# Batch norm, inference form: phases of three tiles instead of two, parameters loaded as rows, and stores held back in four phases

## The chip, the cores and the metric

The kernel runs on one core of a Trainium2 chip. The metric is device time in microseconds (us) of one execution; a median of several is quoted. Every execution below ran at a granted clock of 1.0, all the timed ones were in the fast state, and the single run of `before_again` has the state "unknown", as single runs have. Spreads are quoted.

## The reference

```
x: [32, 256, 128, 128] float32;  gamma, beta, running_mean, running_var: [256] float32
return gamma * (x - running_mean) / sqrt(running_var + 1e-5) + beta      # per channel
```

The input has 537 MB, and so has the output. With scale = gamma / sqrt(var + eps) and shift = beta - mean * scale, each element needs one multiply and one add.

## The kernel before

A tile is 128 channels of one image: 128 partitions x 16384 floats, 8.39 MB, 64 KiB for each partition. There are 64 tiles and three buffers in SBUF. All loads and stores are issued from the sync queue (SP); VectorE works in place. After three first loads the program goes in phases of two: two stores, two loads.

```python
    for i in range(NBUF):                      # NBUF = 3
        issue_load(i)

    def load_param(ap_1d):                     # 256 values, scattered in pieces of 4 bytes
        t = params.tile([P, NCB], mybir.dt.float32, tag=ap_1d.tensor.name)
        nc.gpsimd.dma_start(out=t, in_=ap_1d.rearrange("(j p) -> p j", p=P))
        return t
    # ... four such loads; sqrt on ScalarE, then scale and shift on VectorE [cut]

    K = NBUF - 1
    for b in range((NT + K - 1) // K):
        idxs = [i for i in range(K * b, K * b + K) if i < NT]
        for i in idxs:
            compute(i)                         # one tensor_scalar, in place
        for i in idxs:
            store(i)
        for i in idxs:
            issue_load(i + NBUF)               # waits until the buffer's store is done
```

Of the kernel before, what the change touches and what calls it, by code (L numbers as in the profile page):

```python
# [1 line left out]

# [4 lines left out]


SINGLE_QUEUE = True  # L10
NBUF = 3


@with_exitstack
def kernel(
    ctx: ExitStack,
    tc: tile.TileContext,
    x: bass.AP,
    gamma: bass.AP,
    beta: bass.AP,  # L20
    running_mean: bass.AP,
    running_var: bass.AP,
    out: bass.AP,
):
    nc = tc.nc
    eps = 1e-5

    N, C, H, W = x.shape
    P = nc.NUM_PARTITIONS
    assert C % P == 0  # L30
    NCB = C // P
    HW = H * W
    NT = N * NCB

    params = ctx.enter_context(tc.tile_pool(name="params", bufs=1))
    data = ctx.enter_context(tc.tile_pool(name="data", bufs=NBUF))

    xr = x.rearrange("n (cb p) h w -> (n cb) p (h w)", p=P)
    outr = out.rearrange("n (cb p) h w -> (n cb) p (h w)", p=P)

    tiles = {}
    loads = {}

    def issue_load(i):
        if i >= NT:
            return
        t = data.tile([P, HW], mybir.dt.float32, tag="t")
        loads[i] = nc.sync.dma_start(out=t[:], in_=xr[i])  # L48
        tiles[i] = t

    for i in range(NBUF):
        issue_load(i)

    def load_param(ap_1d):
        t = params.tile([P, NCB], mybir.dt.float32, tag=ap_1d.tensor.name)
        nc.gpsimd.dma_start(out=t, in_=ap_1d.rearrange("(j p) -> p j", p=P))  # L56
        return t

    var_t = load_param(running_var)
    gamma_t = load_param(gamma)  # L60
    beta_t = load_param(beta)
    mean_t = load_param(running_mean)

    eps_t = params.tile([P, 1], mybir.dt.float32, tag="eps")
    nc.vector.memset(eps_t, eps)  # L65

    scale_t = params.tile([P, NCB], mybir.dt.float32, tag="scale")
    shift_t = params.tile([P, NCB], mybir.dt.float32, tag="shift")
    tmp_t = params.tile([P, NCB], mybir.dt.float32, tag="tmp")

    nc.scalar.activation(  # L71
        out=tmp_t[:],
        in_=var_t[:],
        func=mybir.ActivationFunctionType.Sqrt,
        bias=eps_t[:],
        scale=1.0,
    )
    nc.vector.reciprocal(out=tmp_t[:], in_=tmp_t[:])  # L78
    nc.vector.tensor_mul(out=scale_t[:], in0=gamma_t[:], in1=tmp_t[:])  # L79
    nc.vector.tensor_mul(out=tmp_t[:], in0=mean_t[:], in1=scale_t[:])  # L80
    nc.vector.tensor_sub(out=shift_t[:], in0=beta_t[:], in1=tmp_t[:])  # L81

    def compute(i):
        t = tiles[i]
        cb = i % NCB
        nc.vector.tensor_scalar(  # L86
            out=t[:],
            in0=t[:],
            scalar1=scale_t[:, cb : cb + 1],
            scalar2=shift_t[:, cb : cb + 1],  # L90
            op0=mybir.AluOpType.mult,
            op1=mybir.AluOpType.add,
        )

    def store(i):
        t = tiles.pop(i)
        (nc.sync if SINGLE_QUEUE else nc.scalar).dma_start(out=outr[i], in_=t[:])  # L97

    K = NBUF - 1
    for b in range((NT + K - 1) // K):  # L100
        idxs = [i for i in range(K * b, K * b + K) if i < NT]
        for i in idxs:
            compute(i)
        for i in idxs:
            store(i)
        for i in idxs:
            issue_load(i + NBUF)


# [1 line left out]
_INS = ['x', 'gamma', 'beta', 'running_mean', 'running_var']  # L111
_OUTS = [((32, 256, 128, 128), 'float32')]


# [23 lines left out]
```

## Time and profile before

| | before |
|---|---|
| median of the first 3 runs | 2491.8 us (2489.71 to 2493.32) |
| span of the profiled run | 2488.1 us |
| moved | 1073.75 MB, mean 432 GB/s |
| VectorE busy | 23% |

From the page of the kernel before: the span, busy time, the DMA row and its rate in 40 slices of about 62 us, the main DMA queue (packets, MB, share of 16 engines' time), and the one costly group of instructions.

```profile
span 2488.1 us, 378 instructions
DVE 564.7 (23%) x69; ACT 1.6 (0%) x2; POOL 3.2 (0%) x8
...
DMA  9999999999999999999999999999999999999998
GB/s 414 429 438 433 433 429 437 436 430 431 435 436 433 428 437 436 434 428 436 433 437 428 435 435 435 426 437 436 435 427 435 436 438 426 434 437 436 432 431 378
...
q1 hardware_dynamic: 18432, 1073.75, 99.8%
...
L86 DVE TENSOR_SCALAR t<-t,scale_t,shift_t 128x16384 f32<-128x16384 f32 x64 | 564.0, 8812 | 1868.0 <-DMA t<-in_x_dram 1867.9
```

The DMA engines are busy throughout. VectorE needs 8.8 us for a tile and the DMA engines 19.3 us for each of its two transfers, so the idle 1868 us of VectorE cost nothing. The Trainium skill, page "DMA: Bandwidth & Descriptors", section "Where 436 GB/s comes from", gives 435.2 GB/s as the ceiling of the 16 ports into SBUF; the mean of 432 and the best slices of 438 (a slice holds a few packets too many or too few) agree with it.

The timeline of the first two phases (start us, duration us, engine or queue, line):

```profile
0.74 1.33 SPq L48 DMA_DIRECT2D t<-in_x_dram  x3
...
25.56 8.81 DVE L86 TENSOR_SCALAR t<-t,scale_t,shift_t 128x16384 f32<-128x16384 f32 x1
34.40 19.06 SPq L97 DMA_DIRECT2D out_dram<-t  x2
...
82.93 19.66 SPq L48 DMA_DIRECT2D t<-in_x_dram  x2
102.63 28.19 SPq L97 DMA_DIRECT2D out_dram<-t  x2
```

The first two stores are issued at 34 and 53 us, while the loads before them run until about 62 us. Work is always queued well ahead of the engines. Parameters that are ready only at 25.5 us delay nothing.

### How the small losses are read

The page cannot resolve 0.1%. The trace also holds a record of each packet (start, duration, bytes). A packet here is 64 KiB, the share of one partition. The records do not name the DMA engine, so packets were chained: each is put after the packet that ended as it started, which gives 16 chains, one for each engine. (Where two packets end in the same few ns, two chains may be swapped; sums over all chains are not touched by that, but a figure of the worst chain can be off by half a microsecond.) The median packet takes 2.418 us, 2.414 from start to start, so a chain of 1024 packets needs 2472 us. What a chain takes beyond 2.414 us per 64 KiB is called its loss. "Turn" is the point where a chain goes from loads to stores or back.

### The profile page before, as it was taken

To read this page: it belongs to the slowest core of one execution; us is meant where nothing else is said; L and a number is where in the kernel's file an instruction comes from. 1 tells how busy PE (TensorE), PEld (TensorE's weight loads), DVE (VectorE), ACT (ScalarE), POOL (GpSimd) and SP (SyncE) were. 2 spreads that over 40 slices of the span, in tenths; PEclk is the share of its full clock that TensorE was granted. 3 is DMA by queue.
4 is the path that set the end of the run, shared out by engine and by line. 5 is a ranking of instruction groups with operands and counts; after the bars stand their busy time and mean duration, and the time that the engine had idled before them with its cause. 6 is when DMAs were issued, how large, how long until landed. Compare 5 with 4: busy or idle time off the path is not lost.

```text
span 2488.1 us, 378 instructions
## 1 busy us (share of the span) xinstructions
DVE 564.7 (23%) x69; ACT 1.6 (0%) x2; POOL 3.2 (0%) x8
## 2 busy tenths in 40 slices
DVE  2122211222112221122212222121221212212121
ACT  0000000000000000000000000000000000000000
POOL 0000000000000000000000000000000000000000
DMA  9999999999999999999999999999999999999998
GB/s 414 429 438 433 433 429 437 436 430 431 435 436 433 428 437 436 434 428 436 433 437 428 435 435 435 426 437 436 435 427 435 436 438 426 434 437 436 432 431 378
DMA packets 18562, 1073.77 MB, mean 432 GB/s; under 512 B 2176, under 2 KB 2176, under 8 KB 2176
## 3 DMA queue, kind: packets, MB, share of 16 engines
q1 hardware_dynamic: 18432, 1073.75, 99.8%
q0 software_dynamic: 128, 0.00, 0.0%
q14 instruction: 2, 0.02, 0.0%
HBM read 536.88 MB, written 536.87 MB: 432 GB/s over the span
## 4 chain that ended last, share of the span: by engine, by line
DMA 51%; another core or an unknown queue 36%; DVE 11%; SPq 0%; issue 0%; POOL 0%; DVEq 0%; POOLq 0%; PEldq 0%
DMA t<-in_x_dram 48%; DVE t L86 11%; DMA out_dram<-t 2%; DMA t<-in_running_mean_dram 1%; SPq L97 0%; POOL t L56 0%; DVEq L86 0%; POOLq L133 0%; SPq L48 0%; DVE shift_t L81 0%; DVE tmp_t L80 0%; DVEq L80 0%; PEldq L133 0%
## 5 line engine op out<-in xcount | busy, mean ns | idle before, releaser
L86 DVE TENSOR_SCALAR t<-t,scale_t,shift_t 128x16384 f32<-128x16384 f32 x64 | 564.0, 8812 | 1868.0 <-DMA t<-in_x_dram 1867.9
L78 DVE RECIPROCAL tmp_t<-tmp_t 128x2 f32<-128x2 f32 x1 | 0.2, 166 | 13.2 <-ACT tmp_t L71 13.2
L80 DVE TENSOR_TENSOR tmp_t<-t,scale_t 128x2 f32<-128x2 f32 x1 | 0.2, 160 | 7.6 <-DMA t<-in_running_mean_dram 7.6
L71 ACT ACT_TABLE_LOAD x1 | 1.3, 1283 | 12.4 <-DMA t<-in_running_var_dram 12.4
L79 DVE TENSOR_TENSOR scale_t<-t,tmp_t 128x2 f32<-128x2 f32 x1 | 0.2, 160 | 3.2 <-DMA t<-in_gamma_dram 3.2
L56 POOL DMA_DIRECT2D t<-in_running_var_dram x1 | 0.8, 839 | 0.8 <-PEq L133 0.8
L56 POOL DMA_DIRECT2D t<-in_gamma_dram x1 | 0.7, 722 | 0.0
L56 POOL DMA_DIRECT2D t<-in_beta_dram x1 | 0.7, 722 | 0.0
L56 POOL DMA_DIRECT2D t<-in_running_mean_dram x1 | 0.7, 722 | 0.0
L71 ACT ACTIVATE tmp_t<-t,eps_t 128x2 f32<-128x2 f32 x1 | 0.3, 295 | 0.0
L65 DVE MEMSET eps_t<- 128x1 f32 x1 | 0.1, 59 | 0.8 <-PEq L122 0.8
L81 DVE TENSOR_TENSOR shift_t<-t,tmp_t 128x2 f32<-128x2 f32 x1 | 0.2, 160 | 0.0
L122 POOL MEMSET const-bfloat16-1.0<- 128x1 bf16 x1 | 0.1, 96 | 0.0
L122 POOL MEMSET const-uint8-127<- 128x1 uint8 x1 | 0.1, 94 | 0.0
L122 POOL MEMSET const-float32-0.0<- 128x1 f32 x1 | 0.1, 93 | 0.2 <-issue 0.2
L122 POOL MEMSET const-float32-1.0<- 128x1 f32 x1 | 0.1, 93 | 0.0
## 6 DMA issues: line engine op xcount, KB each, us to landing
t<-in_x_dram SPq DMA_DIRECT2D x64, 38.6
out_dram<-t SPq DMA_DIRECT2D x64, 49.9
t<-in_running_var_dram POOLq DMA_DIRECT2D x1, 1.0 KB, 11.1
t<-in_gamma_dram POOLq DMA_DIRECT2D x1, 1.0 KB, 15.2
t<-in_beta_dram POOLq DMA_DIRECT2D x1, 1.0 KB, 19.5
t<-in_running_mean_dram POOLq DMA_DIRECT2D x1, 1.0 KB, 21.6
```

The lines of the kernel that those rows point to most:

```text
L56: nc.gpsimd.dma_start(out=t, in_=ap_1d.rearrange("(j p) -> p j", p=P))
L65: nc.vector.memset(eps_t, eps)
L71: nc.scalar.activation(out=tmp_t[:], in_=var_t[:], func=mybir.ActivationFunctionType.Sqrt, bias=eps_t[:], scale=1.0,)
L78: nc.vector.reciprocal(out=tmp_t[:], in_=tmp_t[:])
L79: nc.vector.tensor_mul(out=scale_t[:], in0=gamma_t[:], in1=tmp_t[:])
L80: nc.vector.tensor_mul(out=tmp_t[:], in0=mean_t[:], in1=scale_t[:])
L81: nc.vector.tensor_sub(out=shift_t[:], in0=beta_t[:], in1=tmp_t[:])
L86: nc.vector.tensor_scalar(out=t[:], in0=t[:], scalar1=scale_t[:, cb : cb + 1], scalar2=shift_t[:, cb : cb + 1], op0=mybir.AluOpType.mult, ...
L122: nc = _bacc.Bacc("TRN2", target_bir_lowering=False, num_devices=1)
```

## The change

Its intent is to turn less often between reading and writing HBM (phases of three tiles use all three buffers), to load the parameters as four rows and transpose them on VectorE, and, in four of 22 phases, to keep the first store back until the DMA engine that lags has nearly finished the phase's loads.

```diff
+GROUPS = [3] * 20 + [2, 2]
+LAST = 3072
+HELD = (5, 10, 15, 20)
...
+    def load_group(g, first):
+        last = first + GROUPS[g] - 1
+        for i in range(first, last):
+            load(i, [HW])
+        if g not in HELD:
+            load(last, [HW])
+            return None
+        return load(last, [HW - LAST, HW])[0]      # 13312 columns, then 3072
...
-        nc.gpsimd.dma_start(out=t, in_=ap_1d.rearrange("(j p) -> p j", p=P))
+    rows = params.tile([B, C], f32, tag="rows")
+    nc.vector.memset(rows, 0.0)
+    for r, ap in enumerate((running_var, gamma, beta, running_mean)):
+        nc.scalar.dma_start(out=rows[r : r + 1, :], in_=ap.rearrange("(o c) -> o c", o=1))
+    # ... nc.vector.transpose and four small copies [cut]
...
+    for g, size in enumerate(GROUPS):
+        idxs = range(first, first + size)
+        for i in idxs:
+            compute(i)
+        for i in idxs:
+            s = store(i)
+            if i == first and gate is not None:
+                tc.add_manual_dep(s.ins, gate.ins.name, after, reason="stores after loads")
+        first += size
+        if g + 1 < len(GROUPS):
+            gate = load_group(g + 1, first)
```

More of the change, by code (lines that the diff above doesn't have):

```diff
@@ L7 @@
 from concourse._compat import with_exitstack
-SINGLE_QUEUE = True
 NBUF = 3
+GROUPS = [3] * 20 + [2, 2]
+LAST = 3072
+HELD = (5, 10, 15, 20)
 @with_exitstack
@@ L26 @@
     eps = 1e-5
+    f32 = mybir.dt.float32
     N, C, H, W = x.shape
@@ L33 @@
     NT = N * NCB
+    B = 32
+    NQ = P // B
+    assert sum(GROUPS) == NT and max(GROUPS) <= NBUF
     params = ctx.enter_context(tc.tile_pool(name="params", bufs=1))
@@ L39 @@
     outr = out.rearrange("n (cb p) h w -> (n cb) p (h w)", p=P)
+    ctx.enter_context(tc.manual_schedule())
     tiles = {}
-    loads = {}
-    def issue_load(i):
-        if i >= NT:
-            return
-        t = data.tile([P, HW], mybir.dt.float32, tag="t")
-        loads[i] = nc.sync.dma_start(out=t[:], in_=xr[i])
-        tiles[i] = t
-    for i in range(NBUF):
-        issue_load(i)
-    def load_param(ap_1d):
-        t = params.tile([P, NCB], mybir.dt.float32, tag=ap_1d.tensor.name)
-        nc.gpsimd.dma_start(out=t, in_=ap_1d.rearrange("(j p) -> p j", p=P))
-        return t
@@ L59, with load @@
-    var_t = load_param(running_var)
-    gamma_t = load_param(gamma)
-    beta_t = load_param(beta)
-    mean_t = load_param(running_mean)
-    eps_t = params.tile([P, 1], mybir.dt.float32, tag="eps")
-    nc.vector.memset(eps_t, eps)
-    scale_t = params.tile([P, NCB], mybir.dt.float32, tag="scale")
-    shift_t = params.tile([P, NCB], mybir.dt.float32, tag="shift")
-    tmp_t = params.tile([P, NCB], mybir.dt.float32, tag="tmp")
+    def load(i, cuts):
+        t = data.tile([P, HW], f32, tag="t")
+        tiles[i] = t, cuts
+        return [
+            nc.sync.dma_start(out=t[:, a:b], in_=xr[i][:, a:b])
+            for a, b in zip([0, *cuts], cuts)
+        ]
@@ new lines @@
+    gate = load_group(0, 0)
+    eps_t = params.tile([P, 1], f32, tag="eps")
+    nc.vector.memset(eps_t, eps)
+    turned = params.tile([B, C], f32, tag="turned")
+    nc.vector.transpose(out=turned[:], in_=rows[:])
+    par = params.tile([P, NCB, 4], f32, tag="par")
+    blocks = turned.rearrange("p (cb q r) -> p cb q r", cb=NCB, q=NQ)
+    for q in range(NQ):
+        nc.vector.tensor_copy(out=par[q * B : (q + 1) * B], in_=blocks[:, :, q, 0:4])
+    var_t, gamma_t, beta_t, mean_t = (par[:, :, r] for r in range(4))
@@ L71 @@
+    scale_t = params.tile([P, NCB], f32, tag="scale")
+    shift_t = params.tile([P, NCB], f32, tag="shift")
+    tmp_t = params.tile([P, NCB], f32, tag="tmp")
     nc.scalar.activation(
         out=tmp_t[:],
-        in_=var_t[:],
+        in_=var_t,
         func=mybir.ActivationFunctionType.Sqrt,
@@ L78 @@
     nc.vector.reciprocal(out=tmp_t[:], in_=tmp_t[:])
-    nc.vector.tensor_mul(out=scale_t[:], in0=gamma_t[:], in1=tmp_t[:])
-    nc.vector.tensor_mul(out=tmp_t[:], in0=mean_t[:], in1=scale_t[:])
-    nc.vector.tensor_sub(out=shift_t[:], in0=beta_t[:], in1=tmp_t[:])
+    nc.vector.tensor_mul(out=scale_t[:], in0=gamma_t, in1=tmp_t[:])
+    nc.vector.tensor_mul(out=tmp_t[:], in0=mean_t, in1=scale_t[:])
+    nc.vector.tensor_sub(out=shift_t[:], in0=beta_t, in1=tmp_t[:])
     def compute(i):
-        t = tiles[i]
+        t, cuts = tiles[i]
         cb = i % NCB
-        nc.vector.tensor_scalar(
-            out=t[:],
-            in0=t[:],
-            scalar1=scale_t[:, cb : cb + 1],
-            scalar2=shift_t[:, cb : cb + 1],
-            op0=mybir.AluOpType.mult,
-            op1=mybir.AluOpType.add,
-        )
-    def store(i):
-        t = tiles.pop(i)
-        (nc.sync if SINGLE_QUEUE else nc.scalar).dma_start(out=outr[i], in_=t[:])
-    K = NBUF - 1
-    for b in range((NT + K - 1) // K):
-        idxs = [i for i in range(K * b, K * b + K) if i < NT]
+        for a, b in zip([0, *cuts], cuts):
+            nc.vector.tensor_scalar(
+                out=t[:, a:b],
+                in0=t[:, a:b],
+                scalar1=scale_t[:, cb : cb + 1],
+                scalar2=shift_t[:, cb : cb + 1],
+                op0=mybir.AluOpType.mult,
+                op1=mybir.AluOpType.add,
+            )
+    def store(i):
+        t, _ = tiles.pop(i)
+        return nc.sync.dma_start(out=outr[i], in_=t[:])
+    after = mybir.DependencyInfo(mybir.DependencyClass.Sync, mybir.DependencyReason.DATA)
+    first = 0
+    for g, size in enumerate(GROUPS):
+        idxs = range(first, first + size)
         for i in idxs:
@@ L104 @@
         for i in idxs:
-            store(i)
-        for i in idxs:
-            issue_load(i + NBUF)
+            s = store(i)
[4 more added lines that the diff above has]
+            gate = load_group(g + 1, first)
 _INS = ['x', 'gamma', 'beta', 'running_mean', 'running_var']
```

## The prediction

> **What bounds the kernel now.** DMA, end to end. The page shows VectorE busy 23% and the DMA row at 9 tenths in all but the last slice; q1 takes 99.8% of 16 engines' time, 1073.75 MB at a mean of 432 GB/s over 2488.1 us. The Trainium skill, "DMA: Bandwidth & Descriptors", section "Where 436 GB/s comes from", puts the ceiling at 435.2 GB/s; this trace agrees (432 mean, best slices 438). Only the distance to that ceiling can be won.
>
> I read it from the packet records. Chaining each 64 KiB packet to the one that ended as it started gives 16 chains of about 1024 packets. The median packet takes 2.418 us (2.414 from start to start), so 1024 need 2472 us. The first starts at 1.8 us, the last ends at 2486.9: the worst chain loses about 13 us (0.5%), in two places:
> - 1.5 to 3.2 us in the first tile, whose packets take up to 4.7 us while the queue starts and the parameter packets pass (7 to 24 us);
> - about 10 us at turns from loads to stores: the last read packet before a turn takes up to 3.15 us, in some chains. One of the 32 turns costs the worst chain about 0.33 us on average. Turns from stores to loads cost almost nothing. Chains drift apart to 9.8 us.
>
> **What the change does.**
> - Three-tile phases: 22 such turns instead of 32. Estimate: 10 x 0.33 = 3.3 us less. The queue stays filled: a 19.3 us transfer covers the 8.8 us tensor_scalar (timeline).
> - Parameters as rows over the scalar queue, turned on VectorE: ready before the present 25.4 us (timeline, shift_t). Worth nothing in itself, as stores queue behind the three first loads (about 60 us); other small packets beside the first tile may save about 1 us.
> - Four held phases: the first store waits for the first 13312 columns of the last tile. The last engine still has 8 packets of 12 KiB then, about 3.6 us (3072/16384 of 19.3), against about 0.5 us from landing to a waiter's start plus 1 to 1.5 us from issue to first packet (0.74 to 1.76 us at the start). So the last engine should not idle; the leaders do, by up to their lead. That realigns the engines but gives the last one nothing back. As another engine may be last afterwards, the sum of the worst of each block (10.9 us in this trace cut into blocks at the holds) replaces the worst sum (9.9 us): about +1 us, less if aligned turns are cheaper.
> - Extra tensor_scalar pieces, SP waits, smaller packets: off the critical path.
>
> **Prediction.** -3.3 - 1 + 1 = -3.3 us on 2491.8: 2488.5 us, ratio 0.9987; range 2480 to 2495. Faster by over 2%: 0.01, within 2%: 0.98, slower by over 2%: 0.01. Over 2% would need more than the packets' own time allows.
>
> **What would show it.** Right: median packet still 2.418 us; DMA row at 9 throughout; late packets at 22 turns only, worst chain losing about 7 us there; shift_t ready before 20 us; the spread between chains dropping at the four holds, with idle time on leaders only. Wrong in size: rarer turns cost more each, or aligned turns nothing (nearer 2480).
>
> **What would make it wrong.** A hold that reaches the last engine too (a gap of 1 to 3 us, four times), a three-tile phase that empties the queue while SP waits for a buffer (a repeated dip of the DMA row), or packet times that change with the length of a run of reads or writes.

## The result, and the profile after

| | before | after |
|---|---|---|
| median, same rounds (and the 3 runs of before) | 2490.76 us (2485.85 to 2493.40, 6 runs) | 2492.29 us (2491.14 to 2493.93, 6 runs) |
| ratio after / before | | 1.0012, 95% interval 1.0001 to 1.0023 |
| span of the profiled run | 2488.1 us | 2489.8 us |

A ratio is the mean time of one kernel's runs over that of the other's in the same rounds, so it is not quite the ratio of the medians. By a difference whose interval only just leaves 1 out, the change did not gain the 3.3 us predicted: it lost about 1.5.

From the page after, the lines that answer to those above, and the new queue of the parameter rows:

```profile
span 2489.8 us, 388 instructions
DVE 566.7 (23%) x79; ACT 1.6 (0%) x2; POOL 0.2 (0%) x4
...
GB/s 421 432 427 438 438 433 426 438 436 434 428 437 432 427 436 434 437 426 437 436 426 425 433 437 437 430 431 438 422 438 421 437 432 430 437 437 434 426 431 397
...
q1 hardware_dynamic: 19008, 1073.75, 99.9%
...
q10 hardware_dynamic: 8, 0.00, 0.0%
```

The page says "full" as before: a late packet counts as busy. The few slices of 421 to 426 in the second half are a hint, no more.

The timeline after, at the start:

```profile
0.73 1.33 SPq L56 DMA_DIRECT2D t<-in_x_dram  x3
...
1.14 0.50 ACTq L74 DMA_DIRECT2D rows<-in_running_var_dram  x1
...
22.38 0.43 DVE L81 STREAM_TRANSPOSE turned<-rows 32x256 f32<-32x256 f32 x1 [21.25 <-DMA rows<-in_running_mean_dram]
```

The four rows of 1 KB land only at about 22 us, although they were issued by 2.5 us. Their eight packets (four of 1024 bytes, four of 4 bytes for the semaphore) start at 4.8, 7.3, 9.7, 12.1, 14.6, 17.0, 19.4 and 21.9 us: one for each 64 KiB packet of the tile loads. The Trainium skill, page "DMA: Bandwidth & Descriptors", section "Queues, rings and completion order", says that an engine goes round its queues packet by packet; the trace agrees, at 2.4 us a round.

The waits of the sync queue after (who waited for what: us in total, times, longest):

```profile
SPq L120 <- DVE t L109: 1228.6, 57, 47.1
SPq L56 <- DMA out_dram<-t: 962.8, 60, 19.1
SPq L120 <- DMA t<-in_x_dram: 214.0, 4, 53.7
```

The third line is the four holds. Now the first tensor_scalar of each phase, in the timeline of VectorE after. Its start is the moment when the phase's first load has landed on all engines, so the distance of two such lines is the length of a phase of three loads and three stores. The phase that begins at 1769.35 is held.

```profile
1653.25 8.81 DVE L109 TENSOR_SCALAR t<-t,scale_t,shift_t 128x16384 f32<-128x16384 f32 x1 [68.48 <-DMA t<-in_x_dram]
...
1769.35 8.81 DVE L109 TENSOR_SCALAR t<-t,scale_t,shift_t 128x16384 f32<-128x16384 f32 x1 [68.53 <-DMA t<-in_x_dram]
...
1885.84 8.81 DVE L109 TENSOR_SCALAR t<-t,scale_t,shift_t 128x16384 f32<-128x16384 f32 x1 [72.40 <-DMA t<-in_x_dram]
...
2003.58 8.81 DVE L109 TENSOR_SCALAR t<-t,scale_t,shift_t 128x16384 f32<-128x16384 f32 x1 [68.56 <-DMA t<-in_x_dram]
...
2119.75 8.81 DVE L109 TENSOR_SCALAR t<-t,scale_t,shift_t 128x16384 f32<-128x16384 f32 x1 [68.46 <-DMA t<-in_x_dram]
```

The phases take 116.10, 116.49 (held), 117.74 and 116.17 us. The held phase is nearly as short as the others; the one **after** it is 1.6 us longer. The same stands at the two holds before: 116.43 then 117.22, and 116.41 then 117.80.

The packet chains show the same in more detail. Loss of the mean chain, in us, at each hold of the changed kernel, and the time from the issue of the first held store to its first packet on the first and on the last chain:

```
hold   issue to first packet     at the held   next turn,      next turn,
       first chain  last chain   turn          stores->loads   loads->stores
1         1.6         3.2          0.07          0.25            0.82
2         0.9         3.2          0.36          0.57            1.13
3         0.8         3.2          0.68          0.68            1.28
4         0.8         3.2          0.42          0.68            1.23
```

Other turns from stores to loads lose 0.01 us, other turns from loads to stores about 0.1 us, but the very first one 1.03 us. The twelve entries add up to 8.2 of the 12.9 us that the mean chain loses.

Read chain by chain, the third hold shows more. The three chains that came last still had 2.2 to 3.2 us of loads before them when the stores were issued, and lost less than 0.1 us at the held turn: they did not run dry. At the next turn to loads they lost 0.01 us, but at the next turn to stores 1.7 to 1.9 us, more than any other chain. On every chain these two turns together cost 1.7 to 2.3 us. At the first hold no chain ran dry at all (all had 1.6 to 3.2 us left), and the two turns still cost the mean chain 1.1 us. So the later loss is not paid only by engines that stood idle.

### The profile page after: what moved, and what is told of

It is laid out like the page before. It is cut to its first block, busy times and chain, and to the rows that moved or that the text cites. A ratio compares the mean times of both kernels' runs of the same rounds, so it can differ in the third digit from the quotient of the medians.

```text
span 2489.8 us, 388 instructions
## 1 busy us (share of the span) xinstructions
DVE 566.7 (23%) x79; ACT 1.6 (0%) x2; POOL 0.2 (0%) x4
## 4 chain that ended last, share of the span: by engine, by line
another core or an unknown queue 72%; DVE 22%; issue 2%; DMA 2%; DVEq 0%; SPq 0%
DVE t L109 22%; DMA t<-in_x_dram 2%; DVEq L109 0%; SPq L56 0%
## 5 line engine op out<-in xcount | busy, mean ns | idle before, releaser
L109 DVE TENSOR_SCALAR t<-t,scale_t,shift_t 128x16384 f32<-128x16384 f32 (+2 forms) x68 | 564.7, 8310 | 1869.8 <-DMA t<-in_x_dram 1817.1
```

Source lines behind the costliest of these rows:

```text
L109: nc.vector.tensor_scalar(out=t[:, a:b], in0=t[:, a:b], scalar1=scale_t[:, cb : cb + 1], scalar2=shift_t[:, cb : cb + 1], op0=mybir.AluOpT ...
```

## The experiments

**Theory.** The hold costs, through lateness: the held stores reach engines that have no queued work left, or nearly none, and after so late a start about 1 us is lost at the next turn from loads to stores, as at the first turn of the changed kernel. **Rivals:** the cut load and its short packets cost; the gate costs whatever its lead; the loss belongs to three-tile phases; and, for the gain that was predicted, turns do cost in proportion to their number (the prediction) or do not. A further rival was not put to a run: engines that a hold has drawn together turn all at once and hinder one another. The trace of the changed kernel speaks against it: at its second turn to stores the chains are 0.8 us apart, closer than after any hold (1.6 us or more), and the mean chain loses 0.04 us.

Four kernels in each of three calls ran on the same chip (chips 1, 7 and 2 in turn) beside the same runs of the kernel before. A difference between calls therefore holds the chip as well. The table gathers all: medians of time, and from one trace of each the loss in us of the mean chain (in the first three tiles, later, and in all), of the worst chain, and how far apart the chains end.

```
kernel           time (lowest-highest)        ratio     first 3  later  mean   worst  ends apart
before           (33 runs, see below)                   2.3      5.1    7.4    13.1   9.2
after            2492.29 (2491.14-2493.93)    1.0012    1.7     11.2   12.9    14.7   2.4
call 1, before 2489.98 (2485.23-2492.58)
no_holds         2487.03 (2486.00-2488.17)    0.9992    1.7      3.7    5.4     8.5   4.8
split_only       2486.31 (2485.08-2486.55)    0.9988    2.0      3.6    5.6     9.0   5.6
all_held         2496.11 (2494.34-2496.74)    1.0027    1.4     15.6   17.0    18.6   3.0
rows_only        2486.45 (2486.02-2486.76)    0.9989    2.0      3.8    5.8     9.5   5.5
call 2, before 2487.24 (2486.41-2492.20)
gate_early       2486.36 (2486.08-2487.16)    0.9998    1.9      5.0    6.9     9.0   3.9
gate_late        2497.26 (2495.99-2498.95)    1.0041    1.7     16.8   18.6    19.1   0.8
hold_loads       2496.05 (2494.77-2496.89)    1.0036    1.9     14.7   16.5    19.0   2.8
one_tile         2487.24 (2485.88-2488.30)    0.9998    1.8      3.8    5.7    11.1   7.5
call 3, before 2487.55 (2486.77-2492.27)
before_again     2491.10 (one run)                      2.3      5.6    7.9    14.0   9.1
scatter_scalar   2500.09 (2499.34-2501.77)    1.0050   12.8      7.5   20.3    24.1   5.8
rows_gpsimd      2486.66 (2485.99-2487.25)    0.9994    1.8      3.8    5.6     9.0   5.5
late_params      2487.16 (2486.97-2492.24)    1.0000    2.3      3.8    6.1    10.1   6.2
```

### no_holds

```diff
-HELD = (5, 10, 15, 20)
+HELD = ()
```

> The changed kernel without any held phase (three-tile phases and row parameters stay). Turn theory of the prediction: about 3 to 4 us under the kernel before, ratio about 0.9985, about 1 us under the changed kernel. Hold-cost theory, from the changed kernel's trace (the held turn plus the two turns after it lose about 1.1, 2.1, 2.6 and 2.3 us on the mean chain, some 8 us in all, where unheld turns lose 0.1): about 2484 us, 7 to 8 us under the changed kernel, and no turn after the first with a mean loss over 0.4 us.

2487.03 us, 5.3 us under the changed kernel's median (other rounds; against the kernel before, 0.9992 instead of 1.0012). The timeline of VectorE in the same five phases as above:

```profile
1651.25 8.81 DVE L109 TENSOR_SCALAR t<-t,scale_t,shift_t 128x16384 f32<-128x16384 f32 x1 [68.43 <-DMA t<-in_x_dram]
...
1767.34 8.81 DVE L109 TENSOR_SCALAR t<-t,scale_t,shift_t 128x16384 f32<-128x16384 f32 x1 [68.56 <-DMA t<-in_x_dram]
...
1883.29 8.81 DVE L109 TENSOR_SCALAR t<-t,scale_t,shift_t 128x16384 f32<-128x16384 f32 x1 [68.47 <-DMA t<-in_x_dram]
...
1999.64 8.81 DVE L109 TENSOR_SCALAR t<-t,scale_t,shift_t 128x16384 f32<-128x16384 f32 x1 [68.47 <-DMA t<-in_x_dram]
...
2115.60 8.81 DVE L109 TENSOR_SCALAR t<-t,scale_t,shift_t 128x16384 f32<-128x16384 f32 x1 [68.39 <-DMA t<-in_x_dram]
```

The phases take 116.09, 115.95, 116.35 and 115.96 us: no long phase. At the same twelve turns the mean chain loses 0.9 us in all, against 8.2 with the holds. That difference of 7.3 is nearly the whole difference of the mean chains (12.9 - 5.4 = 7.5). The time differs by less, because the holds bring the chains together: they end 2.4 us apart instead of 4.8.

### split_only

```diff
-        return load(last, [HW - LAST, HW])[0]
+        load(last, [HW - LAST, HW])
+        return None
```

> The last load of the same four phases cut into 13312 and 3072 columns, but the stores not held. If the hold (the late stores) is what costs: as the kernel without holds, within 1.5 us, and the turns after the cut loads lose about 0.1 us. If the short 12 KiB packets or the extra transfer cost: as the changed kernel, with the losses of 0.3 to 1.3 us in the two turns after each cut.

2486.31 us, like the kernel without holds. The turns at the cut loads and the next ones to stores lost 0.03 to 0.26 us on the mean chain. The cut and the short packets cost nothing that shows here; the wait does.

### all_held

```diff
-HELD = (5, 10, 15, 20)
+HELD = tuple(range(22))
```

> All 22 phases held. Hold-cost theory with a cost of about 2 us per hold: 18 more holds, some 30 to 40 us over the changed kernel, ratio about 1.013 to 1.017. If the cost is one of drifting back into step after a hold and does not add up when every turn is held: under 12 us more. If holds cost only what the prediction said (the worst of the block): within 4 us of the changed kernel.

2496.11 us: 9 us over the kernel without holds, in the same rounds, and only 4 us over the changed kernel. So holds cost, but not by a fixed sum each: 22 of them cost 9 us, four cost 5. In this trace the turns from stores to loads lose 7.4 us in all (no_holds: 0.1) and those from loads to stores about 3 us, so the turns of about 1 us are gone where the next turn is itself held. The estimate of 30 to 40 us was wrong. By its figure alone the run fits the second and just the third of the outcomes written down; the third, that holds cost no more than the prediction said, is excluded by the 9 us over the kernel without holds. In this trace an expensive turn to stores follows a hold only where it is not held itself.

### rows_only

```diff
 # the kernel before, with
-    var_t = load_param(running_var)    # and gamma, beta, mean, through gpsimd
+    for r, ap in enumerate((running_var, gamma, beta, running_mean)):
+        nc.scalar.dma_start(out=rows[r : r + 1, :], in_=ap.rearrange("(o c) -> o c", o=1))
+    # ... transposed as in the change
```

> The kernel before with the parameters as rows and nothing else changed. Prediction: about 1 us faster than before, the first tile losing about 0.7 us on the mean chain instead of 2.2. Rival: the loss of 1.0 us at the first turn from loads to stores that the changed kernel has and the kernel before has not comes with the rows, so that nothing is gained: the same within 0.5 us, with a first turn that loses about 1 us.

2486.45 us, within 0.7 us, against a kernel before that spread over 7 us in the same rounds (median 2489.98; interval of the ratio 0.9975 to 1.0002, so a gain is not proved by these rounds alone). Two things follow. First, two-tile phases with rows are as fast as three-tile phases with rows and no holds (2486.45 and 2487.03): the longer phases bring nothing. Second, half of the rival came true: the first tile loses 0.8 us instead of 2.2, but the first turn then loses 1.18 instead of 0.04, so that the first three tiles lose 2.0 instead of 2.3.

### gate_early

```diff
-LAST = 3072
+LAST = 8192
```

> The changed kernel with the gate moved forward: the four held stores wait for the first 8192 columns of the last load, so that some 9.7 us of reads (estimate: half of 19.3 us) are still queued when they are issued, about 8 us of them when the first store packets could start. Late-store theory (the engines run out of queued work, or nearly, and start anew): no loss at the holds, as without holds, 2486 to 2488 us. Rival, that the gate itself or the stores' later order costs, whatever its lead: as the changed kernel, about 5 us over the kernel without holds, with turns of about 1 us after each hold.

2486.36 us. The gate is the same, the stores still wait for the loads, but at the holds they are issued 7.9, 6.5, 5.7 and 5.3 us ahead of their first packet. The wait of the sync queue; the issue of the third group of held stores, first in the changed kernel, then here; and two phases (the one at 1767.83 held):

```profile
SPq L120 <- DMA t<-in_x_dram: 189.6, 4, 47.6
```

```profile
1804.41 9.39 SPq L120 DMA_DIRECT2D out_dram<-t  x3
```

```profile
1796.86 14.61 SPq L120 DMA_DIRECT2D out_dram<-t  x3
```

```profile
1767.83 8.81 DVE L109 TENSOR_SCALAR t<-t,scale_t,shift_t 128x16384 f32<-128x16384 f32 x1 [68.42 <-DMA t<-in_x_dram]
...
1883.91 8.81 DVE L109 TENSOR_SCALAR t<-t,scale_t,shift_t 128x16384 f32<-128x16384 f32 x1 [72.81 <-DMA t<-in_x_dram]
...
1999.86 8.81 DVE L109 TENSOR_SCALAR t<-t,scale_t,shift_t 128x16384 f32<-128x16384 f32 x1 [68.47 <-DMA t<-in_x_dram]
```

116.08 and 115.95 us: no time is lost, and the turns after the holds lose 0.03 to 0.23 us. The rival that the gate costs whatever its lead falls.

### gate_late

```diff
-LAST = 3072
+LAST = 1024
```

> The same with the gate at 15360 of 16384 columns, so that about 1.2 us of reads are left: every engine, the last one too, runs dry at the four holds. Late-store theory: the same kind of loss as in the changed kernel and somewhat more, 1 to 2 us more per hold of plain idle time less what the near-dry holds already lost, 2493 to 2498 us in all. Rival as above: as the changed kernel.

2497.26 us, 10.9 us over gate_early in the same rounds, with nothing changed but where the last load is cut. At all four holds the first packet comes 0.8 us after the issue on the first chain and 1.0 us on the last: every engine had run dry. (The median 4 KiB packet of the cut takes 0.16 us, 0.01 more than its share of a 64 KiB packet, which makes less than 0.1 us a hold; so the shorter packets are not the reason.) The issue of the third group of held stores, and the phases:

```profile
1809.51 9.39 SPq L120 DMA_DIRECT2D out_dram<-t  x3
```

```profile
1772.01 8.81 DVE L109 TENSOR_SCALAR t<-t,scale_t,shift_t 128x16384 f32<-128x16384 f32 x1 [68.50 <-DMA t<-in_x_dram]
...
1889.51 8.81 DVE L109 TENSOR_SCALAR t<-t,scale_t,shift_t 128x16384 f32<-128x16384 f32 x1 [70.96 <-DMA t<-in_x_dram]
...
2006.48 8.81 DVE L109 TENSOR_SCALAR t<-t,scale_t,shift_t 128x16384 f32<-128x16384 f32 x1 [68.67 <-DMA t<-in_x_dram]
```

Now the held phase is long too (117.50 us, the idle time), and the next 116.97. The next turns lose 0.8 us (stores to loads) and 0.7 to 1.2 us (loads to stores). The chains are drawn together completely, to 0.8 us at the end, and the kernel is still some 10 us slower than the one without holds (other rounds).

### hold_loads

```diff
 # no_holds, with
+HELD_LOADS = (5, 10, 15, 19)
+            s = store(i, [HW - LAST, HW] if held and i == idxs[-1] else [HW])
+            if held:
+                tc.add_manual_dep(made[0].ins, s[0].ins.name, after, reason="loads after stores")
```

> The mirror image: three-tile phases, no store held, but in four phases the next loads wait for the first 13312 columns of the phase's last store. Start-anew theory (a nearly empty queue costs its own 0.1 to 0.7 us and then about 1 us at the next turn from loads to stores, as the first turn after the kernel's start does): again some 5 us over the kernel without holds, each held turn followed by a turn to stores that loses about 1 us on all chains. Rival, that it is peculiar to stores held behind loads: no such turn, within 2 us of the kernel without holds.

2496.05 us, more than was expected: 9 us over the kernel without holds (other rounds).

```profile
1772.64 8.81 DVE L105 TENSOR_SCALAR t<-t,scale_t,shift_t 128x16384 f32<-128x16384 f32 x1 [68.75 <-DMA t<-in_x_dram]
...
1889.41 8.81 DVE L105 TENSOR_SCALAR t<-t,scale_t,shift_t 128x16384 f32<-128x16384 f32 x1 [69.21 <-DMA t<-in_x_dram]
...
2006.90 8.81 DVE L105 TENSOR_SCALAR t<-t,scale_t,shift_t 128x16384 f32<-128x16384 f32 x1 [68.56 <-DMA t<-in_x_dram]
```

The held turn, at the end of the phase that begins at 1772.64, makes that phase 116.77 us long, and the next one takes 117.49. In the chains the next turn to stores loses 0.98, 1.16, 1.19 and 1.30 us on the mean chain. So the effect is not peculiar to held stores: whichever side is late, the next turn from loads to stores costs about 1 us.

### one_tile

```diff
 # rows_only, with
-    K = NBUF - 1        # and the loop over phases of two
+    for i in range(NT):
+        compute(i)
+        store(i)
+        if i >= 1:
+            issue_load(i - 1 + NBUF)
 # and tc.manual_schedule(), as in the changed kernel [cut]
```

> Row parameters, and loads and stores taking turns tile by tile: 62 turns from loads to stores instead of 32 or 22, with the queue always filled. The prediction's term (about 0.1 us on the mean chain and 0.33 us on the worst chain for each turn): some 3 us on the mean and up to 10 us on the worst chain more than with 32 turns, 2489 to 2497 us. Rival, suggested by 32 and 22 turns having cost the same (3.9 and 3.7 us on the mean chain): the count of turns does not matter, within 1.5 us of 2486.5 us.

2487.24 us with 62 turns to stores; the mean chain loses 4.2 us at them, against 3.9 us at 32 turns (rows_only) and 3.7 us at 22 (no_holds). Most of that falls in the first turns: 1.17 us in the first, 0.9 in the next three together, 0.017 each in the last thirty. The times do not follow the number of turns, and that was the prediction's main term. A small dependence is not excluded: on the worst chain, which is what the prediction reckoned with, the turns cost 6.9, 7.5 and 9.8 us at 22, 32 and 62 turns (one trace each, read by chaining), so at most 0.08 us for each added turn and not 0.33.

### before_again

No edit.

> The kernel before once more, unchanged, for a second trace of it. Its times spread over 8 us (2485.2 to 2493.4) where five kernels with row parameters and no near-empty queue lay between 2485.1 and 2488.3. If the spread is one of how far the 16 chains drift apart: a trace with a time near 2486 shows chains that end less than 6 us apart, one near 2492 shows about 10 us as the first trace did; the loss of the mean chain stays near 7 us in both.

2491.1 us, with chains that end 9.1 us apart, as in the first trace. The lower case did not come up, so the tie between time and drift is supported from one side only. The 33 timed runs of the kernel before lie in two groups: 20 between 2485.2 and 2487.6 us, 13 between 2489.3 and 2493.4. How often the upper one comes up differs between the calls: 6 of 9 runs in call 1, 1 and 2 of 9 in the others. All 30 runs of the six kernels with rows and well-fed queues (rows_only, no_holds, split_only, gate_early, one_tile, rows_gpsimd) lie between 2485.1 and 2488.3. What the rows take away is the upper group, and a few tenths of a microsecond besides.

### scatter_scalar

```diff
-        nc.gpsimd.dma_start(out=t, in_=ap_1d.rearrange("(j p) -> p j", p=P))
+        nc.scalar.dma_start(out=t, in_=ap_1d.rearrange("(j p) -> p j", p=P))
```

> The kernel before with its four parameter loads issued from the scalar queue, in the same scattered form of 4 byte elements. If the queue (gpsimd) is what costs: as the kernel with rows only, 2486 to 2487.5 us with little spread. If the many small packets cost: 2489 to 2493 us or more, with a first tile that loses 2 us or more.

2500.09 us: the small packets cost, far more than was thought, but not where it was expected (the first tile was to lose 2 us or more). From the DMA issues of this kernel (KB, us from issue to landing), and its timeline:

```profile
t<-in_running_var_dram ACTq DMA_DIRECT2D x1, 1.0 KB, 41.8
t<-in_gamma_dram ACTq DMA_DIRECT2D x1, 1.0 KB, 61.0
```

```profile
63.04 26.26 DVE L86 TENSOR_SCALAR t<-t,scale_t,shift_t 128x16384 f32<-128x16384 f32 x3
71.88 9.07 SPq L97 DMA_DIRECT2D out_dram<-t  x2
```

The 4 byte packets of this queue take turns with the 64 KiB packets, so that the parameters land when the three tile loads are over. By the packet records the scalar queue moved the four parameters in 1024 packets of 4 bytes, gpsimd in 64 of 64 bytes. The first store is issued at 71.9 us and the queue stands empty for 11 us (the first turn loses 11.4 us). No gate is in this kernel, yet after its late stores the next two turns lose 0.8 and 1.3 us on the mean chain, as after a hold. The run says what late parameters cost, but the first tile loses only 0.75 us, so it does not tell why the gpsimd form sets the chains apart.

### rows_gpsimd

```diff
 # rows_only, with
-        nc.scalar.dma_start(out=rows[r : r + 1, :], ...)
+        nc.gpsimd.dma_start(out=rows[r : r + 1, :], ...)
```

> Row parameters as in the changed kernel, but issued from gpsimd, on the two-tile kernel. If the queue costs: as the kernel before, median 2488 to 2492 us with a spread of several us, and a first tile that loses about 2 us. If the form costs: as rows only, 2486 to 2487 us.

2486.66 us, as with rows from the scalar queue. For rows the queue makes no difference that shows, so it is the form of the loads that counts; the first tile loses 0.70 us.

### late_params

```diff
+        tc.add_manual_dep(d.ins, loads[0].ins.name, after, reason="parameters after the first tile")
```

> The kernel before with its gpsimd parameter loads held until the first tile has landed (the first store is still queued well before the loads run out at about 61 us). If it is the meeting of parameter packets with the first tile's packets that costs and sets the chains apart: the first tile loses 0.6 to 0.8 us, the first turn to stores about 1.1 us, and the time is 2486 to 2487.5 us. If loading the parameters by small gpsimd packets costs wherever it stands: as before, 2488 to 2492 us.

Four runs between 2486.97 and 2487.22 us and one of 2492.24. The first tile now loses 0.66 us and the first turn only 0.09, but the loss reappears in the second tile, beside which the packets now pass: the first three tiles lose 2.3 us as before. So the small packets shift a loss of about 2 us about within the first three tiles; and with one run of five in the upper group, moving them does not settle what sets the chains apart. That stays open.

## Why the prediction was right or wrong

The time fell inside the range (2480 to 2495), and "within 2%" was right: the bound by DMA packet time held, with a median packet of 2.418 us before and after. The direction was wrong: -3.3 us was forecast, +1.5 us measured (ratio 1.0012, interval 1.0001 to 1.0023). The largest term failed whole, and the cost of the holds was about five times what was forecast. That the sum still came within 4 us of the forecast is in part luck: the turns were 3.3 us too hopeful and the holds about 4, while the rows, in call 1, gave 2.5 us more than was counted on.

- **"22 such turns instead of 32. Estimate: 10 x 0.33 = 3.3 us less."** This step failed. A sum over 32 turns was divided by 32 and multiplied by 10, as if each turn cost alike. With rows and no late work, 62, 32 and 22 turns cost the mean chain 4.2, 3.9 and 3.7 us, and the times are 2487.24, 2486.45 and 2487.03 us. In the times the term measures about 0; on the worst chain of the traces, 0.6 us between 32 and 22 turns (7.5 and 6.9).
- **"Other small packets beside the first tile may save about 1 us."** Right in sign, and in size it depends on the rounds: 3.5 us of the median in call 1, 0.9 us in call 3 (rows_gpsimd), because the kernel before has two groups of times and the rows leave the lower one. The reason given, the first tile, was wrong: what it gains there it loses at the first turn.
- **"About +1 us, less if aligned turns are cheaper"** for the holds. Mis-sized: about +5 us. The prediction looked for the cost at the held turn itself, and was right there: the last engine does not idle (its first store packet starts 3.2 us after the issue, and the three chains that come last lose less than 0.1 us at the third hold), the leaders do, and the spread falls. Most of the cost came at the two turns afterwards, 1.1 to 2.0 us on the mean chain at each hold, also on chains that had not idled. gate_early against gate_late shows the cause on one chip: the same gate is free when the stores are issued 5 us or more ahead and costs 10.9 us with all else alike when the engines run dry. (The changed kernel itself lies between them, in other rounds.)
- **"Ready before 20 us"** for shift_t: wrong, 24.6 us. The rows wait a round of 64 KiB packets eight times. It cost nothing, as was said.
- **"A hold that reaches the last engine too"** was named as the danger, with a gap at the hold. The danger was real and the place was wrong: no gap, but a longer phase after.

The sum with measured terms: rows -3.5 (call 1), phases about 0, holds +5.3, together about +1.8 us against +1.5 measured. The terms come from different rounds, so the closeness should not be pressed.

What stays open: why, after stores or loads that came late, about 1 us is lost at the next turn from loads to stores, when later turns cost a tenth of that; why the chains that did not run dry pay it too; and why some executions of the kernel before drift apart by 9 us. No run here opens the DMA engine.

No kernel beats the field: no_holds, split_only, rows_only, gate_early and rows_gpsimd all lie at 2486.3 to 2487.0 us, some 5 to 6 us (0.2%) under the changed kernel. The simplest of them is the kernel before with parameter rows.

## What to carry to other kernels

When the DMA engines are full, keep work queued several microseconds ahead of them at every turn; here a gate meant to line engines up was free with 5 us of lead or more and cost 1 to 3 us each time with about 3 us or less (what lies between was not tried), and most of the bill came a phase later, where nobody looks. Lining engines up did not pay: of the 7.5 us that the holds cost the mean chain it gave back about 2 in the time, and the kernel whose engines ended closest together (0.8 us) was among the slowest. Before multiplying a "cost per event" by a changed number of events, look at whether the events cost alike; here the first few turns carried most of it.

## What the Trainium skill lacked or had wrong

- "DMA: Bandwidth & Descriptors" has no cost for a queue that runs dry, or nearly, in a long stream. Here each hold of the changed kernel cost the mean chain 1.1 to 2.6 us, most of it at the next two turns, and 5 us of lead made it nothing.
- The same page has no cost of turning between reading and writing HBM. Here a turn from loads to stores cost the mean chain about 0.1 us (0.7 to 1.3 us after a late issue, and 1.0 to 1.3 us when it was the first after the start in a kernel with rows), and one from stores to loads 0.01 us (0.3 to 0.8 us after late stores).
- The same page, section "Latency and other measured facts", gives about 600 ns to the first byte for a DMA issued from sync or scalar. It does not say from which moment. Here, on empty engines, 0.8 to 1.0 us passed from the start of the issuing instruction to the first packet, and 0.5 to 0.65 us from its end (the instruction takes 0.34 us), so the figure fits if it is counted from the end.
- The same page, section "Issuing engine by pattern", says that DMAs from sync and scalar are generally faster than those from gpsimd. For 1 KB scattered in 4 byte pieces beside large loads it was the reverse: 42 to 61 us to landing from the scalar queue (1024 packets of 4 bytes), 11 to 22 us from gpsimd (64 packets of 64 bytes).
- No page warns that a small DMA beside 64 KiB packets waits a whole packet for each of its own: here 2.4 us for each, about 20 us for four rows of 1 KB. The rule of turns that explains it is there, under "Queues, rings and completion order".
